# A third width of pass for the small experts of a mixture-of-experts decoder layer, with bias rows loaded first and other edits

## The chip, the cores and the metric

The kernel runs on one core of one Trainium2 chip. The metric is the device time of one execution in microseconds; the median of three runs of the kernel before is 1851.08 us (1849.51 to 1851.67).

## The reference

One decoder layer over 512 tokens of width 1024: a token mixer (an mLSTM branch and a latent-attention branch, gated and merged), cross-attention into 256 memory tokens, and a mixture of experts, each followed by a LayerNorm of `alpha * x + f(x)`. The change lies in the mixture of experts and in the last LayerNorm. Cut to that:

```python
logits = x @ w_router + b_router                    # 512 x 32 experts
top_val, top_idx = top_k(logits, 4);  gate = softmax(top_val)
for each expert e, over the tokens that chose it:
    gu  = x_e @ w_gu[e] + b_gu[e]                   # 1024 -> 2048, two halves: gate and linear
    glu = min(gu_gate, 7);  lin = clip(gu_lin, -7, 7)
    act = glu * sigmoid(1.702 * glu) * (lin + 1)
    y[tokens] += gate_e * (act @ w_dn[e] + b_dn[e]) # 1024 -> 1024
out = layer_norm(alpha * x + y) * ln3_g + ln3_b
```

All weights are float32. How many tokens an expert gets depends on the data and is known only at run time.

## The kernel before, in words

The kernel runs the dense part (mixer, attention, router) first, to about 600 us, then the experts one after the other (`experts`, L1250 to L1347), to about 1811 us, then the last LayerNorm (`finish`, L1465).

Weights. An expert has 24 slabs of 512 KB: 16 for up (8 slices of 128 input channels, by two halves, gate and linear) and 8 for down. SP issues their loads in the order of their use (`slab`, L186) into a ring of 36 buffers: 3 (`raw`) and 6 (`whi`, `wlo`) that the dense part used before, and 8, 14 and 5 more (`NRAW`). A load is issued when its buffer is free, so SP runs ahead of the matmuls by up to 36 slabs.

Tokens. An expert's tokens stand in slots 0 to 191. GpSimd gathers their rows from DRAM (128 into `xg`, up to 64 more into `mrxg`); `tokens` transposes them on TensorE and ScalarE copies them to `xe` (64, then 64 if there are over 64, then 64 if over 128). Over 192 tokens go another way (`overflow`), which these data don't need.

Passes. TensorE holds the tokens as the stationary operand and streams the weights, 512 columns a matmul. A pass is one sweep over some slabs for a group of slots. A pass of 64 slots puts two matmuls side by side on two column tiles of 64; a pass of 32 slots puts four on four column tiles of 32 (`four`, and `down_32`). In float32 each matmul of the program appears as two MATMUL and two LDWEIGHTS records, and each pass of eight matmuls as x16.

`up` (L1104 to L1127) works through four quarters of two slices each. In every quarter there is a pass for slots 0 to 63, and then, nested in conditions on the count `rv`, slots 64 to 95 (L1119), 96 to 127 (L1121) and 128 to 191 (L1123):

```python
self.up_part(e, ks, 64, x[:, :, 0:64], w, two(b))
with tc.If(rv > 64):
    self.up_part(e, ks, 32, x[:, :, 64:96], w, four(b[2]))
    with tc.If(rv > 96):
        self.up_part(e, ks, 32, x[:, :, 96:128], w, four(b[3]))
        with tc.If(rv > 128):
            self.up_part(e, ks, 64, x[:, :, 128:192], w, two(bm))
```

In the last quarter each pass also adds the bias rows by a matmul (`bias`, L1090) with `bgu`, a split of the biases into three bfloat16 parts. `down` (L1182) has two halves of four slices each, nested in the same way (L1189, L1191, L1193). `hidden` turns the activated rows back (L1153 to L1168, conditions at L1162 and after).

Order. The order of the work on TensorE, VectorE, ScalarE and GpSimd is written out by hand (`manual_schedule`). In round e: up of expert e; behind its first quarter `hidden` of expert e-1, behind its third quarter the slots of expert e+2 (`route_expert`, small matmuls on `sl`, L1007 and L1010); then down of expert e-1, in whose middle the activation of expert e (`units`, on VectorE and ScalarE) and the token transposes of expert e+1 stand, with the gather for e+2; then `rows_out` of expert e-1 (VectorE and ScalarE write the result to one of two buffers `ysb`, GpSimd scatters and adds it to `based` in DRAM, L1031). SP's loads are not in that order by hand; they follow the ring.

Conditions. PE's sequencer executes a condition as a compare-and-branch, which the profile shows at the line after the `If` (L1119, L1189 and so on) as PEldq. If the arm is skipped, the sequencer jumps over its instructions.

Start of the stretch. SP issues 24 slabs, then the eight loads of the bias rows (`bias_rows`, L1230), then the other slabs. VectorE and ScalarE turn them into `bgu`, with seven steps one after the other per half. ScalarE's queue also issues the last four stores of `based` (L1048), and ScalarE makes the first token copy.

End. `finish` loads `based` in four blocks; each block's LayerNorm takes sums with bn_stats and bn_aggr on VectorE (L661, L662), the root on GpSimd, a scaling on ScalarE (L667), and two products and two additions by halves (L669, L670); the additions of blocks 0 and 2 run on GpSimd (`FP`), the others on VectorE.

Of the kernel before, what the change touches and what calls it, by code (L numbers as in the profile page):

```python
# [9 lines left out]
F32 = mybir.dt.float32  # L10
# [101 lines left out]
class Trunk:  # L112
# [541 lines left out]

    def layer_norm(self, z, out, gb, add=None, keep=False):

        nc = self.nc
        st = self.pst.tile([128, 2, 6], F32, name="bn", tag="bn")
        mv = self.pst.tile([128, 4], F32, name="mv", tag="mv")
        for i in range(2):  # L660
            nc.vector.bn_stats(st[:, i, :], half(z, i))  # L661
        nc.vector.bn_aggr(mv[:, 0:2], st)  # L662
        self.rstd_col(mv[:, 2:3], mv[:, 1:2])
        nc.vector.scalar_tensor_tensor(mv[:, 3:4], mv[:, 0:1], -1.0, mv[:, 2:3], op0=OP.mult, op1=OP.mult)
        for i in range(2):
            v = half(z, i)
            nc.scalar.activation(v, v, AF.Identity, bias=mv[:, 3:4], scale=mv[:, 2:3])  # L667
            u = half(out, i) if keep else v
            nc.vector.tensor_mul(u, v, half(gb[0], i))  # L669
            (add or nc.vector).tensor_add(half(out, i), u, half(gb[1], i))  # L670

# [401 lines left out]
    def tokens(self, rv):  # L1073

        nc, tc = self.nc, self.tc
        x = self.mx.tile([128, 8, 192], F32, name="xe", tag="xe", bufs=1)

        def some(c, n, src, first=0):
            nc.scalar.copy(x[:, :, c:c + n], self.turned(src, 8, "xt", first).rearrange("p (k t) -> p k t", t=n))  # L1079

        some(0, 64, self.xg[0:64])
        with tc.If(rv > 64):  # L1082
            some(64, 64, self.xg[64:128], 64)
            with tc.If(rv > 128):
                some(128, 64, self.more_x)
        return x
# [17 lines left out]
    def up(self, rv, e, x, w, between):  # L1104

        tc = self.tc
        b = [self.ps("gu", "gu") for _ in range(4)]
        bm = [self.ps("gux", "y") for _ in range(2)]

        def two(b):  # L1110
            return lambda h, j: b[j][64 * h:64 * h + 64]

        def four(b):
            return lambda h, j: b[64 * j + 32 * h:64 * j + 32 * h + 32]

        for q in range(4):
            ks = (2 * q, 2 * q + 1)
            self.up_part(e, ks, 64, x[:, :, 0:64], w, two(b))
            with tc.If(rv > 64):  # L1119
                self.up_part(e, ks, 32, x[:, :, 64:96], w, four(b[2]))  # L1120
                with tc.If(rv > 96):  # L1121
                    self.up_part(e, ks, 32, x[:, :, 96:128], w, four(b[3]))
                    with tc.If(rv > 128):  # L1123
                        self.up_part(e, ks, 64, x[:, :, 128:192], w, two(bm))
            for work in between.get(q, ()):
                work()
        return b, bm  # L1127
# [9 lines left out]
    def units(self, rv, b, bm, twice, between):  # L1137

        tc = self.tc
        g = self.mx.tile([128, 512], F32, name="mg", tag="mg", bufs=1)  # L1140
        l, l2, lx = [self.mx.tile([128, 512], F32, name=n, tag=n, bufs=1) for n in ("ml", "ml2", "mlx")]
        with tc.If(rv > 128):
            self.some_units(g, lx, *bm)
        self.some_units(g, l, b[0], b[1], twice)
        between()
# [6 lines left out]
    def hidden(self, rv, l, l2, lx):  # L1152
# [7 lines left out]

        some(0, 64, l)
        with tc.If(rv > 64):  # L1162
            some(64, 32, l2[0:64])
            with tc.If(rv > 96):  # L1164
                some(96, 32, l2[64:128], 64)
                with tc.If(rv > 128):
                    some(128, 64, lx)
        return hs  # L1168
# [13 lines left out]
    def down(self, rv, h, w, middle):  # L1182
# [3 lines left out]
        for q in range(2):  # L1186
            ks = range(4 * q, 4 * q + 4)
            self.down_64(ks, y, h[:, :, 0:64], w)
            with tc.If(rv > 64):  # L1189
                self.down_32(ks, y2, h[:, :, 64:96], w)  # L1190
                with tc.If(rv > 96):  # L1191
                    self.down_32(ks, y3, h[:, :, 96:128], w)
                    with tc.If(rv > 128):  # L1193
                        self.down_64(ks, yx, h[:, :, 128:192], w)
            if q == 0:
                middle()
        return y, y2, y3, yx

    def rows_out(self, rv, few, p, route):

        nc, tc = self.nc, self.tc
        self.ys.reverse()
        y = self.ys[0]
        yx = self.mx.tile([64, 1024], F32, name="ysx", tag="ysx", bufs=1)
        gate = route[0][1]
# [7 lines left out]

        with tc.If(rv > 64):
            with tc.If(rv > 96):
                with tc.If(rv > 128):
                    for n in range(2):
                        t = yx[:, ts(n, 512)]
                        nc.scalar.copy(t, p[3][64 * n:64 * n + 64])
                        nc.scalar.mul(t, t, route[1][1])  # L1220
                sums(slice(96, 128), p[2])
            sums(slice(64, 96), p[1])
        nc.vector.tensor_copy(y[0:64, 0:512], p[0][0:64])
        nc.scalar.copy(y[0:64, 512:1024], p[0][64:128])  # L1224
        self.scatter(y, route[0][0])
# [3 lines left out]
    def bias_rows(self):  # L1229
# [3 lines left out]
        for h in range(2):  # L1233
            raw = p.tile([128, 2, 512], F32, name="bguraw", tag=("ysx", "hs")[h], bufs=1)
            for i in range(4):
                nc.sync.dma_start(raw[32 * i:32 * i + 32], self.a["bgu"][:, ts(h, 1024)].rearrange("e (j c) -> e j c", j=2))
            nc.vector.tensor_scalar(raw[:, 1], raw[:, 1], 1.0, None, op0=OP.add)
            t = p.tile([128, 2, 512], BF, name="bgu", tag="bgu", bufs=2)
            nc.scalar.copy(t, raw)
            for first in (32, 64):  # L1240
                for r in (slice(a, a + 32) for a in range(first, 96, 32)):
                    nc.vector.tensor_sub(raw[r], raw[r], t[r])
                    nc.scalar.copy(t[r], raw[r])
            self.bgu.append(t)

    def cond(self, c, *engines):
# [3 lines left out]
    def experts(self):  # L1250
        nc, tc, a = self.nc, self.tc, self.a
        p, cond = self.mx, self.cond
        PE, DVE, ACT, POOL = (mybir.EngineType.PE, mybir.EngineType.DVE, mybir.EngineType.Activation, mybir.EngineType.Pool)
        self.more_x = p.tile([64, 1024], F32, name="mrxg", bufs=1)
        nc.vector.memset(self.more_x, 0.0)
        self.ys = [p.tile([128, 1024], F32, name=f"ysb{i}", bufs=1) for i in range(2)]
        for y in self.ys:
            nc.vector.memset(y, 0.0)

# [21 lines left out]
        def more_gather(e):  # L1281
            with tc.If(rv[e][2] > 128):
                self.gather(self.more_x, route[e][1][0])

# [64 lines left out]
    def overflow(self):  # L1349
# [4 lines left out]
        with tc.If(rv > CAP):  # L1354
# [52 lines left out]
            with tc.For_i(0, total, 1):  # L1407
# [52 lines left out]
                y = p.tile([128, 1024], F32, name="oy", tag="ysx", bufs=1)  # L1460
                for n in range(2):
# [3 lines left out]
    def finish(self):  # L1465
        nc, tc, a = self.nc, self.tc, self.a
        with tc.tile_pool(name="fin", bufs=1, reuse_waits="tile") as p:
# [9 lines left out]
    FP = 0, 2  # L1477

    NRAW = 8, 14, 5
    W0, KF, MID = 2, 0, 6  # L1480
# [43 lines left out]
```

## Time and profile before

| | |
|---|---|
| median of 3 runs | 1851.08 us |
| the profiled execution | 1848.75 us, its span 1847.0 us |
| granted TensorE clock, mean of the span | 0.977 |
| PE, matmul | 1673.8 us busy, 91% |
| VectorE | 625.5 us, 34% |
| ScalarE | 469.8 us, 25% |
| GpSimd | 293.9 us, 16% |
| DMA | 504.87 MB, mean 273 GB/s |

The span is the profiled execution from its first instruction to its last; 1.75 us of that execution lie around it. The busy shares are means over the dense part, the experts and the end, which differ: in most of the expert stretch the DMA engines move 350 to 400 GB/s, in the dense part between 69 and 225 for most of it. A row of the timeline gives the start, the busy time, the engine, the line and the tiles, the count of instructions in a run of equal ones, and in brackets the idle time before it with what ended it.

### The profile page before, as it was taken

Reading aid. Unit: us, or ns where it says so; the run is one execution under the profiler, and the core shown is the slowest. Engines: PE = TensorE matmul, PEld = TensorE weight load, DVE = VectorE, ACT = ScalarE, POOL = GpSimd, SP = SyncE. Lnnn points to the kernel's source line nnn. Section 1 sums busy time; section 2 is a strip of 40 time slices with the busy share of each in tenths; the row PEclk is TensorE's granted clock in tenths of the full one; section 3 lists DMA queues with packets and bytes.
Section 4 is the critical chain, followed back from the end, with each engine's and each line's share of the span. In section 5 each row is a group of like instructions: output and inputs, shape, how many; then the busy total and the mean of one; then the engine's idle time right before and its main releaser. Section 6 shows DMA issues by size and latency. Waiting matters only on the chain. (4 is left out here: it accounts for less than half of the span.)

```text
span 1847.0 us, 26521 instructions
## 1 busy us (share of the span) xinstructions
PE 1673.8 (91%) x9564; PEld 853.2 (46%) x9564; DVE 625.5 (34%) x1322; ACT 469.8 (25%) x906; POOL 293.9 (16%) x402
## 2 busy tenths in 40 slices
PE   8999999999999688999999989899999999999991
PEld 7766877868987333333333333333333333333330
DVE  7855777567565411111111211111112102121114
ACT  5577655335443211101101201110101101111001
POOL 1010002421002211211101121111111211011102
PEclk9999999999999799999999999999999999999996
DMA  5223323675236999999858899999999999678973
GB/s 171 91 69 109 105 81 123 221 225 173 83 123 219 351 391 346 396 374 383 305 186 267 325 375 395 364 372 382 392 401 382 376 392 354 229 284 328 399 270 120
DMA packets 149256, 504.87 MB, mean 273 GB/s; under 512 B 21648, under 2 KB 24240, under 8 KB 149040
## 3 DMA queue, kind: packets, MB, share of 16 engines
q1 hardware_dynamic: 131152, 459.33, 66.2%
q0 software_dynamic: 17024, 40.97, 7.6%
q8 instruction: 149, 2.44, 0.5%
q10 hardware_dynamic: 864, 1.57, 0.2%
q14 instruction: 67, 0.55, 0.1%
HBM read 486.84 MB, written 33.29 MB: 282 GB/s over the span
## 5 line engine op out<-in xcount | busy, mean ns | idle before, releaser
L1098 PE MATMUL gu<-raw,xe 128*64 128x512 f32 (+1 forms) x2624 | 518.0, 601 | 27.8 <-PEq L1191 5.1
L1098 PEld LDWEIGHTS gu<-raw,xe 128*64 128x64 f32 (+1 forms) x2624 | 158.2, 127 | 319.8 <-issue 292.9
L1173 PE MATMUL y<-raw,hs 128*64 128x512 f32 x920 | 211.1, 597 | 17.1 <-PEq L1121 4.3
L1133 ACT ACTIVATE mg<-mg 128x512 f32<-128x512 f32 (+1 forms) x55 | 34.7, 630 | 528.8 <-DVE mg L1132 524.4
L1012 DVE TENSOR_REDUCE gs<-sl 128x1 f32<-128x3 f32 x32 | 5.1, 161 | 478.3 <-PE sl L1010 478.3
L998 POOL TENSOR_SCALAR oh<-places,pm 128x192 bf16<-128x192 bf16 x128 | 98.7, 800 | 387.9 <-PE sl L1010 375.8
L1173 PEld LDWEIGHTS y<-raw,hs 128*64 128x64 f32 x920 | 71.1, 136 | 126.5 <-issue 91.1
L130 DVE TENSOR_TENSOR wlo<-raw,whi 128x1024 fp32r<-128x1024 f32 (+2 forms) x81 | 86.9, 1075 | 45.8 <-ACT whi L130 45.3
L1031 POOL DMA_INDIRECT based<-ysb,ixm x32 | 51.5, 1611 | 292.5 <-ACT ysb L1224 280.2
L130 ACT CAST whi<-raw 128x1024 fp32r<-128x1024 f32 (+2 forms) x81 | 75.3, 932 | 81.9 <-issue 17.3
L1098 PE MATMUL gu<-wlo,xe 128*64 128x512 f32 (+1 forms) x368 | 87.5, 594 | 3.1 <-PEq L1164 1.7
L1098 PE MATMUL gu<-whi,xe 128*64 128x512 f32 (+1 forms) x336 | 79.3, 599 | 7.5 <-DVE ysb L1211 2.1
L1025 POOL DMA_INDIRECT xg<-x2d,ixm x32 | 35.9, 1121 | 313.3 <-PEq L1082 179.3
L1132 DVE TENSOR_SCALAR mg<-gu 128x512 f32<-128x512 f32 (+1 forms) x52 | 35.8, 688 | 126.9 <-PE gu L1090 122.8
L1079 ACT COPY xe<-xt 128x512 f32<-128x512 f32 x50 | 27.8, 588 | 190.5 <-PE xt L1070 190.5
L1180 PE MATMUL y<-raw,hs 128*32 128x512 f32 x440 | 57.6, 598 | 0.0
L1211 DVE TENSOR_TENSOR ysb<-ysb,y 32x512 f32<-32x512 f32 x30 | 20.4, 680 | 103.1 <-ACT ysb L1210 103.0
L162 PE MATMUL g<-xTh,wlo 128*128 128x512 f32 x128 | 52.1, 407 | 2.8 <-DVE wlo L130 2.8
L1158 ACT COPY hs<-ht 128x512 f32<-128x512 f32 (+1 forms) x55 | 26.5, 510 | 106.8 <-PEq L1162 56.2
L160 PE MATMUL g<-xTh,whi 128*128 128x512 f32 x128 | 52.2, 408 | 0.0
L161 PE MATMUL g<-xTl,whi 128*128 128x512 f32 x128 | 51.8, 405 | 0.0
L1098 PEld LDWEIGHTS gu<-wlo,xe 128*64 128x64 f32 (+1 forms) x368 | 25.2, 125 | 49.0 <-issue 47.1
(495 smaller groups left out, 2776.9 us busy)
## 6 DMA issues: line engine op xcount, KB each, us to landing
raw<-in_wgu SPq DMA_DIRECT2D x406, 512.0 KB
raw<-in_wdn SPq DMA_DIRECT2D x230, 512.0 KB
wlo<-in_wgu SPq DMA_DIRECT2D x53, 512.0 KB
whi<-in_wgu SPq DMA_DIRECT2D x53, 512.0 KB
raw<-in_wt SPq DMA_DIRECT2D x27, 512.0 KB
whi<-in_wdn SPq DMA_DIRECT2D x13, 512.0 KB
wlo<-in_wdn SPq DMA_DIRECT2D x13, 512.0 KB
tgd<-tg POOLq DMA_DIRECT2D x16, 256.0 KB, 3.5
```

Source lines behind the costliest of these rows:

```text
L130: return nc.scalar.copy(hi, src).ins, (lo_eng or nc.vector).tensor_sub(lo, src, hi.bitcast(F32)).ins
L160: mm(out, w[0], x[0], start=start, stop=False)
L161: mm(out, w[0], x[1], start=False, stop=False)
L162: mm(out, w[1], x[0], start=False, stop=stop)
L998: self.nc.gpsimd.tensor_scalar(oh[:, b], self.places, self.pm[:, b, e:e + 1], None, op0=OP.is_equal)
L1025: return self.nc.gpsimd.indirect_dma_start(out=xg, out_offset=None, in_=self.x2d, in_offset=bass.IndirectOffsetOnAxis(ap=ix[:, 0:1], axis= ...
L1031: self.nc.gpsimd.indirect_dma_start(out=self.based, out_offset=bass.IndirectOffsetOnAxis(ap=ix[:, 0:1], axis=0), in_=y, in_offset=None, bo ...
L1098: mm(out(h, j), x[:, k], w(h, k)[:, ts(j, 512)], start=k == 0, stop=False)
L1132: nc.vector.tensor_scalar(g, pg, 7.0, None, op0=OP.min)
L1133: nc.scalar.activation(g, g, AF.Gelu_apprx_sigmoid)
L1173: self.nc.tensor.matmul(o[64 * n:64 * n + 64], h[:, k], w(k)[:, ts(n, 512)], start=k == 0, stop=k == 7)
L1180: self.nc.tensor.matmul(o[r:r + 32], h[:, k], w(k)[:, ts(n, 512)], start=k < 2, stop=k > 5)
```

## The change

In `up`, `hidden`, `units`, `down` and `rows_out` the work for the first 64 slots now stands in a condition `rv > 32`, with the further conditions nested in it; its other arm handles 32 slots in one pass on four column tiles. Beyond 128 slots, up and hidden go by two groups of 32 (the second under `rv > 160`) instead of one of 64; down still does 64 there. The gather beyond 128 goes to rows 64 to 127 of a tile of 128 rows, `more`, whose rows 0 to 63 take the results beyond 128. There is one `ysb` instead of two. The ring has 38 slabs instead of 36. The bias rows are loaded on ScalarE's queue, ahead of all slabs, the first half into `ysb`. In the last LayerNorm blocks 1 and 3 take their sums on ScalarE, with two activations that accumulate (`sums`), and all additions run on VectorE.

```diff
@@ layer_norm
-        for i in range(2):
-            nc.vector.bn_stats(st[:, i, :], half(z, i))
-        nc.vector.bn_aggr(mv[:, 0:2], st)
+        if stats:
+            stats(mv, z, out)
+        else:
+            for i in range(2):
+                nc.vector.bn_stats(st[:, i, :], half(z, i))
+            nc.vector.bn_aggr(mv[:, 0:2], st)
...
-            (add or nc.vector).tensor_add(half(out, i), u, half(gb[1], i))
+            nc.vector.tensor_add(half(out, i), u, half(gb[1], i))
+
+    def sums(self, mv, z, scratch):
+        nc = self.nc
+        nc.scalar.activation(scratch, z, AF.Identity, accum_out=mv[:, 0:1])
+        nc.vector.tensor_scalar(mv[:, 3:4], mv[:, 0:1], -1.0 / 1024, None, op0=OP.mult)
+        nc.scalar.activation(scratch, z, AF.Square, bias=mv[:, 3:4], accum_out=mv[:, 1:2])
+        nc.vector.tensor_scalar(mv[:, 0:1], mv[:, 3:4], -1.0, None, op0=OP.mult)
+        nc.vector.tensor_scalar(mv[:, 1:2], mv[:, 1:2], 1.0 / 1024, None, op0=OP.mult)
@@ tokens
-                some(128, 64, self.more_x)
+                some(128, 64, self.more[64:128], 64)
@@ up
-            self.up_part(e, ks, 64, x[:, :, 0:64], w, two(b))
-            with tc.If(rv > 64):
-                self.up_part(e, ks, 32, x[:, :, 64:96], w, four(b[2]))
-                with tc.If(rv > 96):
-                    self.up_part(e, ks, 32, x[:, :, 96:128], w, four(b[3]))
-                    with tc.If(rv > 128):
-                        self.up_part(e, ks, 64, x[:, :, 128:192], w, two(bm))
+            with tc.If(rv > 32) as some:
+                self.up_part(e, ks, 64, x[:, :, 0:64], w, two(b))
+                with tc.If(rv > 64):
+                    self.up_part(e, ks, 32, x[:, :, 64:96], w, four(b[2]))
+                    with tc.If(rv > 96):
+                        self.up_part(e, ks, 32, x[:, :, 96:128], w, four(b[3]))
+                        with tc.If(rv > 128):
+                            self.up_part(e, ks, 32, x[:, :, 128:160], w, four(bm[0]))
+                            with tc.If(rv > 160):
+                                self.up_part(e, ks, 32, x[:, :, 160:192], w, four(bm[1]))
+            with some.Else():
+                self.up_part(e, ks, 32, x[:, :, 0:32], w, four(b[0]))
@@ units
         with tc.If(rv > 128):
-            self.some_units(g, lx, *bm)
-        self.some_units(g, l, b[0], b[1], twice)
+            nc.vector.memset(lx[64:128], 0.0)
+            self.some_units(g[0:64], lx[0:64], bm[0][0:64], bm[0][64:128])
+            with tc.If(rv > 160):
+                self.some_units(g[64:128], lx[64:128], bm[1][0:64], bm[1][64:128])
+        with tc.If(rv > 32) as some:
+            self.some_units(g, l, b[0], b[1], twice)
+        with some.Else():
+            self.some_units(g[0:64], l[0:64], b[0][0:64], b[0][64:128])
@@ hidden
-        some(0, 64, l)
-        with tc.If(rv > 64):
...
-                with tc.If(rv > 128):
-                    some(128, 64, lx)
+        with tc.If(rv > 32) as more:
+            some(0, 64, l)
+            with tc.If(rv > 64):
...
+                    with tc.If(rv > 128):
+                        some(128, 32, lx[0:64])
+                        some(160, 32, lx[64:128], 64)
+        with more.Else():
+            some(0, 32, l[0:64])
@@ down
-            self.down_64(ks, y, h[:, :, 0:64], w)
-            with tc.If(rv > 64):
...
+            with tc.If(rv > 32) as some:
+                self.down_64(ks, y, h[:, :, 0:64], w)
+                with tc.If(rv > 64):
...
+            with some.Else():
+                self.down_32(ks, y, h[:, :, 0:32], w)
@@ rows_out
-        self.ys.reverse()
-        y = self.ys[0]
-        yx = self.mx.tile([64, 1024], F32, name="ysx", tag="ysx", bufs=1)
+        y, yx = self.ys, self.more[0:64]
...
+        with some.Else():
+            sums(slice(0, 32), p[0])
@@ bias_rows
-            raw = p.tile([128, 2, 512], F32, name="bguraw", tag=("ysx", "hs")[h], bufs=1)
+            raw = p.tile([128, 2, 512], F32, name="bguraw", tag="hs", bufs=1) if h else self.ys.rearrange("p (j c) -> p j c", j=2)
             for i in range(4):
-                nc.sync.dma_start(raw[32 * i:32 * i + 32], self.a["bgu"][:, ts(h, 1024)].rearrange("e (j c) -> e j c", j=2))
+                nc.scalar.dma_start(raw[32 * i:32 * i + 32], self.a["bgu"][:, ts(h, 1024)].rearrange("e (j c) -> e j c", j=2))
...
+        nc.vector.memset(self.ys, 0.0)
@@ experts
-        self.more_x = p.tile([64, 1024], F32, name="mrxg", bufs=1)
-        nc.vector.memset(self.more_x, 0.0)
-        self.ys = [p.tile([128, 1024], F32, name=f"ysb{i}", bufs=1) for i in range(2)]
-        for y in self.ys:
-            nc.vector.memset(y, 0.0)
+        self.more = p.tile([128, 1024], F32, name="more", bufs=1)
+        self.ys = p.tile([128, 1024], F32, name="ysb", bufs=1)
+        nc.vector.memset(self.more, 0.0)
...
-        fetch(24)
         self.bias_rows()
-        fetch(n - 24)
+        fetch(n)
@@ finish
-                self.layer_norm(z, out[b], gb, nc.gpsimd if b in self.FP else None)
+                self.layer_norm(z, out[b], gb, stats=self.sums if b % 2 else None)
...
-    NRAW = 8, 14, 5
+    NRAW = 8, 14, 7
```

## Rows read from the trace of the kernel before

**Rows 1.** Busy time of the engines over the span (share), instructions.

```profile
PE 1673.8 (91%) x9564; PEld 853.2 (46%) x9564; DVE 625.5 (34%) x1322; ACT 469.8 (25%) x906; POOL 293.9 (16%) x402
```

**Rows 2.** Windows: PE, PEld, DVE, ACT, POOL busy; PE clock, DMA share, GB/s.

```profile
1000.00:1050.00 50.00, 47.02 (x287) 15.78 (x283) 11.61 (x21) 8.84 (x15) 5.91 (x7) 1.00 0.80 286
...
1250.00:1300.00 50.00, 44.86 (x274) 16.55 (x268) 8.64 (x21) 5.24 (x10) 9.87 (x12) 1.00 1.00 383
```

**Rows 3.** PE's waits, what for: us in total, times, longest.

```profile
PE gu L1090 <- ACT bgu L1243: 10.9, 2, 6.6
...
PE ht L1070 <- PEq L1119: 5.0, 16, 0.5
...
PE ht L1070 <- PEq L1121: 4.1, 7, 0.7
...
PE y L1173 <- DMA raw<-in_wdn: 3.1, 8, 0.5
```

**Rows 4.** Timeline of SP's queue, 1440 to 1462 us.

```profile
1455.73 5.70 SPq L186 DMA_DIRECT2D raw<-in_wgu  x4
```

**Rows 5.** Timeline of PE, 1455 to 1490 us.

```profile
1459.68 1.94 PE L1098 MATMUL gu<-whi,xe 128*64 128x512 f32 x8 [0.30 <-DMA raw<-in_wgu]
```

**Rows 6.** Timeline of PE, 1484 to 1500 us.

```profile
1487.14 7.22 PE L1098 MATMUL gu<-raw,xe 128*64 128x512 f32 x48 [0.31 <-PEq L1189]
1494.30 3.65 PE L1098 MATMUL gux<-raw,xe 128*64 128x512 f32 x16
```

**Rows 7.** ScalarE's token copies, from the costliest groups.

```profile
L1079 ACT COPY xe<-xt 128x512 f32<-128x512 f32 x50 | 27.8, 588 | 190.5 <-PE xt L1070 190.5
```

**Rows 8.** Timeline of PE, 1265 to 1330 us.

```profile
1292.95 3.65 PE L1173 MATMUL y<-raw,hs 128*64 128x512 f32 x16
1296.54 1.92 PE L1180 MATMUL y<-raw,hs 128*32 128x512 f32 x16
```

**Rows 9.** Branches at L1119, all and 1092 to 1094: ns min/median/max.

```profile
L1119 PEldq COMPARE_BRANCH  x128: 65/208/3248, 618.0 to 1789.2; - x128
...
L1119 PEldq COMPARE_BRANCH  x1: 3248/3248/3248, 1092.7 to 1092.7; - x1
```

**Rows 10.** Timeline of SP's queue, 530 to 660 us.

```profile
618.74 4.38 SPq L1236 DMA_DIRECT2D bguraw<-in_bgu  x8
```

**Rows 11.** Timeline of ScalarE, 600 to 660 us.

```profile
610.13 4.43 ACTq L1048 DMA_DIRECT2D based<-x2g  x4
614.81 0.59 ACT L1079 COPY xe<-xt 128x512 f32<-128x512 f32 x1 [4.48 <-PE xt L1070]
...
632.89 1.04 ACT L1239 CAST bgu<-bguraw 128x1024 bf16<-128x1024 f32 x1 [17.50 <-DVE bguraw L1237]
```

**Rows 12.** Timeline of GpSimd at the end, 1805 to 1848 us.

```profile
1836.72 3.26 POOL L670 TENSOR_TENSOR fo<-fz,gain 128x512 f32<-128x512 f32 x2 [0.93 <-DVE fz L669]
```

**Rows 13.** Timeline of VectorE at the end, 1810 to 1848 us.

```profile
1838.96 1.58 DVE L670 TENSOR_TENSOR fo<-fz,gain 128x512 f32<-128x512 f32 x1
...
1841.17 0.69 DVE L670 TENSOR_TENSOR fo<-fz,gain 128x512 f32<-128x512 f32 x1
```

**Rows 14.** DMA issues of the scatter: count, median us to landing.

```profile
based<-ysb,ixm POOLq DMA_INDIRECT x32, 9.2
```

**Rows 15.** Timeline of PE, 1088 to 1113 us.

```profile
1092.60 3.65 PE L1098 MATMUL gu<-raw,xe 128*64 128x512 f32 x16 [0.30 <-PEq L1189]
1096.55 1.01 PE L1070 MATMUL ht<-ident,ml 128*128 128x128 f32 x8 [0.30 <-PEq L1119]
```

**Rows 16.** Instruction queue in 650 to 1810, 1093 to 1112, 1094 to 1111: packets, MB, share.

```profile
q8 instruction: 123, 2.02, 0.7%
...
q8 instruction: 4, 0.07, 1.4%
...
q8 instruction: 2, 0.03, 0.8%
```

More of the change, by code (lines that the diff above doesn't have):

```diff
@@ L653, in gains, with layer_norm @@
         return t
-    def layer_norm(self, z, out, gb, add=None, keep=False):
+    def layer_norm(self, z, out, gb, keep=False, stats=None):
         nc = self.nc
@@ L1137, in units @@
     def units(self, rv, b, bm, twice, between):
-        tc = self.tc
+        nc, tc = self.nc, self.tc
         g = self.mx.tile([128, 512], F32, name="mg", tag="mg", bufs=1)
@@ L1159, in some @@
                            self.turned(src, 4, "ht", first).rearrange("p (j h t) -> p j h t", j=4, h=2))
-        some(0, 64, l)
-        with tc.If(rv > 64):
-            some(64, 32, l2[0:64])
-            with tc.If(rv > 96):
-                some(96, 32, l2[64:128], 64)
-                with tc.If(rv > 128):
-                    some(128, 64, lx)
+        with tc.If(rv > 32) as more:
+            some(0, 64, l)
+            with tc.If(rv > 64):
+                some(64, 32, l2[0:64])
+                with tc.If(rv > 96):
+                    some(96, 32, l2[64:128], 64)
+                    with tc.If(rv > 128):
[3 more added lines that the diff above has]
+            some(0, 32, l[0:64])
         return hs
@@ L1187, in down @@
             ks = range(4 * q, 4 * q + 4)
-            self.down_64(ks, y, h[:, :, 0:64], w)
-            with tc.If(rv > 64):
[L1190 to L1194, printed above, removed]
+            with tc.If(rv > 32) as some:
+                self.down_64(ks, y, h[:, :, 0:64], w)
+                with tc.If(rv > 64):
+                    self.down_32(ks, y2, h[:, :, 64:96], w)
+                    with tc.If(rv > 96):
+                        self.down_32(ks, y3, h[:, :, 96:128], w)
+                        with tc.If(rv > 128):
+                            self.down_64(ks, yx, h[:, :, 128:192], w)
+            with some.Else():
+                self.down_32(ks, y, h[:, :, 0:32], w)
             if q == 0:
@@ L1212, in sums @@
             nc.vector.tensor_scalar(y[r], y[r], gate[r], None, op0=OP.mult)
[L1214 to L1224, printed above, removed]
+        with tc.If(rv > 32) as some:
+            with tc.If(rv > 64):
+                with tc.If(rv > 96):
+                    with tc.If(rv > 128):
+                        for n in range(2):
+                            t = yx[:, ts(n, 512)]
+                            nc.scalar.copy(t, p[3][64 * n:64 * n + 64])
+                            nc.scalar.mul(t, t, route[1][1])
+                    sums(slice(96, 128), p[2])
+                sums(slice(64, 96), p[1])
+            nc.vector.tensor_copy(y[0:64, 0:512], p[0][0:64])
+            nc.scalar.copy(y[0:64, 512:1024], p[0][64:128])
+        with some.Else():
+            sums(slice(0, 32), p[0])
         self.scatter(y, route[0][0])
@@ L1282, in more_gather @@
             with tc.If(rv[e][2] > 128):
-                self.gather(self.more_x, route[e][1][0])
+                self.gather(self.more[64:128], route[e][1][0])
         def routing(e):
@@ L1459, in overflow @@
                         nc.tensor.matmul(py[n], h[:, k], w[:, ts(n, 512)], start=k == 0, stop=k == 7)
-                y = p.tile([128, 1024], F32, name="oy", tag="ysx", bufs=1)
+                y = self.ys
                 for n in range(2):
@@ L1473, in finish @@
                 nc.sync.dma_start(z, self.based[ts(b, 128), :])
-                self.layer_norm(z, out[b], gb, nc.gpsimd if b in self.FP else None)
+                self.layer_norm(z, out[b], gb, stats=self.sums if b % 2 else None)
                 nc.sync.dma_start(self.out[ts(b, 128), :], out[b])
-    FP = 0, 2
-    NRAW = 8, 14, 5
+    NRAW = 8, 14, 7
     W0, KF, MID = 2, 0, 6
```

## The prediction, before the change was run

> **What bounds the kernel now.** I read the page's busy times first: TensorE (PE) works in 1673.8 of 1847.0 us, no other engine in over half [rows 1]. [...] PE's waits for the down weights sum to 3.1 us in the whole run, 0.5 at longest; its only long waits are the two for the bias rows, 10.9 us together; the rest are short ones behind its own branches (PEq) [rows 3]. Weights arrive early: SP issues the first up weights of expert 24 at 1455.73, and PE reaches them at 1487.14, 31 us later, a few of which are the transfer itself [rows 4, 6]. I take a lead of 28. So PE sets the pace, and a pass taken away is worth its own time as long as that lead lasts and nothing on PE's queue takes its place.
>
> How long one expert takes is read from starts: expert 23's up begins at 1459.68 and expert 24's at 1487.14, so 27.5 us for an expert of at most 64 tokens [rows 5, 6].
>
> **How often each branch is taken.** The trace shows 50 token copies: 32 first, 15 second, 3 third [rows 7]. So 15 experts have over 64 tokens, 3 of them over 128. How the 17 others split at 32 no row shows; the reference's router, worked out with its inputs, gives six of at most 32 (experts 10, 15, 17, 18, 25, 30) and eleven of 33 to 64, and puts 131, 144 and 147 in the three largest, all under 160.
>
> **What the change takes from PE.** A pass of 64 rows lasts 3.65 us and one of 32 1.92, starts 3.59 apart after the former [rows 8]: 1.73 us a pass. A small expert has six such passes (four in up, two in down): 6 x 6 x 1.73 = 62.3 us. The three largest run their third up pass, 3.65 us as well [rows 6], at 32 rows: 3 x 4 x 1.73 = 20.8.
>
> **What it adds to PE.** Every expert goes through one more branch in seven places (four up quarters, hidden, two down halves). A branch costs about 0.07 us not taken and 0.21 taken (the ends of 65 and 208 ns) [rows 9]. The 26 experts over 32 fall through: 26 x 7 x 0.07 = 12.7. The eleven of 33 to 64 also leave the arm by a jump: waits behind one jump are 0.31 us (5.0/16), behind a nested one 0.58 (4.1/7) [rows 3], so 0.27 x 7 x 11 = 20.8. Small ones jump: 0.21 x 7 x 6 = 8.8. The largest skip the pass beyond 160 (0.56 x 4 x 3 = 6.7) and turn hidden rows in two copies (3). Together 52.
>
> **The bias rows.** Today their eight loads go out on SP at 618.74, behind 24 slabs, ScalarE converts from 632.89, and PE waits 10.9 us for the last of it [rows 3, 10, 11]. Ahead of the slabs they land earlier; but the chain of casts and subtractions keeps its length. I take 8 of the 10.9. The other end is a loss: now ScalarE's queue issues them, 4.38 us of issue today on SP, behind its stores of the base rows (from 610.13, 4.43 us) [rows 10, 11], and ahead of the first token copy, for which PE waits; the two together, some 8 us late, are the bound.
>
> **The end.** GpSimd's last two adds take 3.26 us while the same add on VectorE takes 1.58 beside them and 0.69 alone [rows 12, 13]. Without them VectorE gets four adds more and half the sums less; ScalarE's two full passes lengthen the last block's chain. I take a gain of 2, bounds 3 either way (two of the GpSimd adds' 1.63).
>
> **Edits at nothing.** One output buffer instead of two: a scatter lands 9.2 us (median) after its issue [rows 14], and the shortest expert will still last about 18; were it late, VectorE's writing of the rows would wait, and PE only when the PSUM tiles are wanted again, two halves on. The branches in the units and in the writing of rows run on VectorE and ScalarE beside down passes; two more slabs in the ring only add lead, and SP's later slabs, 4.38 us earlier without the bias loads [rows 10], add to it too.
>
> So far: 62.3 + 20.8 + 8 + 2 - 52 = 41 us gained, 1848.75 - 41 = 1808.
>
> **The term that turns it.** The longest branch record is 3248 ns, at 1092.7, against a median of 208 [rows 9]. It costs nothing today: the pass issued just before it, at 1092.60, runs 3.65 us, and PE is idle 0.30 afterwards [rows 15]. What it waits for shows among the DMA queues: the instruction queue moves 123 pages of 16 KB in 31 experts, 4.0 each, run or skipped; from 1093 to 1112 it moves 4 and without the outer microsecond at both ends 2, so three steps in 17 to 19 us, 5.7 to 6.3 us a page while the weights fill the DMA engines [rows 16]. I take 5.75. The code of an expert grows: up has six passes for four, down five for four, so 6 x 32 + 5 x 16 = 272 matmuls for 192; with transposes and routing unchanged, 4.0 pages become about 5.4, and an expert can't be shorter than 5.4 x 5.75 = 31.1 us. A small one has 27.5 - 10.4 + 1.5 = 18.6 us of work: 12.5 short, 75 over six. One of 33 to 64 has 27.5 + 7 x 0.34 = 29.9: 1.2 short, 13 over eleven. Larger ones have time enough. Gross 88. Off goes what expert 10 would pay, since the DMA share is 0.80 where it runs [rows 2], 12.5, and some 10 for pages in hand where a small one follows a large one. I take 65; the bounds are 0 and 88.
>
> [...]
>
> **The sum:** 1848.75 - 41 + 65 = 1873 for the profiled execution. The median of the runs is 2.3 above that execution, so 1875.
>
> **Rivals.**
> *Pages arrive in time* (the other side). For it: every fetch so far is hidden, and a stalled PE stops taking slabs, so that SP stops issuing and pages come faster. Against it: small experts run through pages in 3.4 us (18.6/5.4), under the 5.7 measured. The time is 1810 against the median. It decides at 18.6/5.4: with a page under 3.4 us nothing is exposed.
> *Pages come at 5.0 us.* The floor is 27, only small ones pay, 8.4 each, five of them, less the 10: 32. Then -41 + 32 = -9: 1842.
> *The full price*, no page in hand: -41 + 88 = +47: 1898.
> *The weights become the bound.* Only where fetches are hidden: experts 15, 17, 18 and 21 to 23 draw faster than the DMA engines refill. An expert is 24 slabs of 512 KB, 12.6 MB, at 383 GB/s [rows 2] 33 us; each small one takes 14 us off the lead of 28, two in a row all of it; some 5 us lost: 1815.
> *It doesn't do what it says*: no expert takes the short arm at run time. Then the 62.3 are gone and the six pay 0.34 instead of 0.21 in seven places: -41 + 62 + 5 = +26: 1877, and more with the fetches.
>
> **How the numbers follow.** A measurement can tell 0.2% (3.7 us). Chances: forecast 0.44 (1858 to 1890), pages in time 0.26, half 0.16 (0.10 of it faster, 0.06 within), full price 0.10, weights 0.03 (0.02 faster, 0.01 within), the last 0.01 (slower). Faster 0.26 + 0.10 + 0.02 = 0.38, same 0.06 + 0.01 = 0.07, slower 0.44 + 0.10 + 0.01 = 0.55. The range reaches from pages in time to the full price, 1807 to 1898; only the outer parts of both lie beyond. The likeliest case's own is 1858 to 1890.
>
> **What would show it.** Right: branch records of several us at the new outer conditions of up and down, PE idle behind them, the instruction queue near 123 x 5.4/4.0 = 166 pages in the expert stretch, small experts about 31 us from start to start, those of 33 to 64 about 30 to 31, passes of 1.92 in the small ones, the bias wait gone down to 3. Wrong: small experts at 19 us, or PE waiting for weights behind experts 18 and 23, or the new branches no longer than 0.21 us.

## The result, and the profile after the change

The changed kernel takes 1916.41 us (median of 4 runs, 1915.08 to 1922.99) against 1850.46 before: a ratio of 1.0362, 95% interval 1.0347 to 1.0377. It is 66 us slower; the prediction had the sign, but 1875 and a range up to 1898.

The page's busy times, clock slices (tenths of full speed, 40 slices) and instruction queue (packets, MB, share):

```profile
PE 1618.4 (85%) x9576; PEld 814.2 (43%) x9576; DVE 629.7 (33%) x1340; ACT 476.2 (25%) x923; POOL 286.8 (15%) x398
...
PEclk9999999999997899999999899997999999999986
...
q8 instruction: 198, 3.24, 0.7%
```

PE has 55 us less to do than before [rows 1], in a span 66 us longer: 121 us of new idle time. What ends it, PE's waits say:

```profile
PE gu L1110 <- DMA raw<-in_wdn: 21.9, 18, 3.2
PE gu L1110 <- DMA raw<-in_wgu: 19.3, 19, 4.3
PE gu L1110 <- issue: 18.6, 24, 3.4
PE gu L1110 <- ACTq L1094: 16.3, 1, 16.3
...
PE y L1201 <- PEq L1133: 7.5, 7, 2.0
...
PE ht L1082 <- PEq L1135: 5.5, 7, 1.1
```

The two largest groups name weights, and one would go looking for a full DMA queue. That is the trap of this profile. Expert 17's up (22 tokens) shows it:

```profile
1302.98 3.64 PE L1110 MATMUL gu<-raw,xe 128*32 128x512 f32 x16 [4.30 <-DMA raw<-in_wgu]
...
1309.33 3.41 PE L1110 MATMUL gu<-raw,xe 128*32 128x512 f32 x16 [1.04 <-DMA raw<-in_wgu]
1315.12 3.03 PE L1110 MATMUL gu<-raw,xe 128*32 128x512 f32 x16 [2.38 <-DMA raw<-in_wdn]
...
1320.87 3.64 PE L1110 MATMUL gu<-raw,xe 128*32 128x512 f32 x16 [1.98 <-DMA raw<-in_wdn]
```

Its up can't be waiting for down weights (`in_wdn`): the named transfers only landed last before the matmul started. The sequencer's branch records say more (minimum, median, maximum in ns; first and last start). L1131 and L1216 stand behind the new condition `rv > 32` in up and in down, L1133 behind `rv > 64`; the last line is L1131 in this stretch alone:

```profile
L1131 PEldq COMPARE_BRANCH  x128: 70/73/6053, 616.1 to 1858.0; - x128
...
L1133 PEldq COMPARE_BRANCH  x148: 65/176/5112, 629.3 to 1862.4; - x148
...
L1216 PEldq COMPARE_BRANCH  x64: 65/73/5482, 682.5 to 1873.7; - x64
...
L1131 PEldq COMPARE_BRANCH  x4: 442/3670/5873, 1296.8 to 1318.9; - x4
```

The branch that starts at 1296.8 lasts 5873 ns, so it ends at 1302.7, and the first matmul follows at 1302.98. The sequencer stood in the jump to the short arm. What it stood for shows in the packets of the instruction queue in the same trace. Pages of 16 KB start at 1300.19, 1305.91, 1312.47, 1318.26 and 1324.00, so 5.7 to 6.6 us apart, four of them within this up:

```profile
q8 instruction: 4, 0.07, 1.3%
```

The three long jumps end at 1302.71, 1314.95 and 1320.71, each 2.5 us after the start of a page. That is no chance: of the 35 branch records over 2 us in the changed kernel every one ends 2.3 to 2.5 us after such a start. The long branches wait for code.

Over the expert stretch 48 branch records exceed 0.7 us, 151.8 us together; before there were 20, 34.9 us together, at most 3248 ns [rows 9].

Three windows of that same up compare its length (columns as in [rows 2]). The changed kernel:

```profile
1302.98:1324.87 21.89, 16.49 (x93) 4.74 (x93) 0.55 (x5) 0.93 (x2) 4.65 (x6) 0.58 1.02 398
```

The same up in the kernel before:

```profile
1299.02:1316.73 17.71, 16.29 (x88) 6.31 (x89) 3.78 (x10) 1.83 (x4) 4.65 (x6) 1.00 1.03 390
```

And in the kernel `e2_all_wide` below, in which this expert runs the wide arm:

```profile
1304.87:1327.28 22.41, 18.37 (x93) 6.57 (x93) 1.28 (x7) 1.44 (x3) 4.65 (x6) 0.92 1.03 398
```

Narrow passes make it 4.2 us longer than before, not 7 us shorter, and wide ones in the same code take half a microsecond more. There, too, the pages of this up come 5.8 us apart, four in its 22.41 us. The granted clock also fell: 0.58 on the mean, 0.50 from 1302.14 to 1312.38 and from 1315.79 to 1326.03, and the passes take 3.0 to 3.6 us, where a pass of expert 18's up, at 1343.12 and a clock of 1.00, takes 1.92. When it fell, at 1302.14, PE had stood idle since 1298.68, the first 3.5 us of the 4.30 before this up.

### The profile page after: what moved, and what is told of

It is laid out like the page before. It is cut to its first block, busy times and chain, and to the rows that moved or that the text cites. A ratio compares the mean times of both kernels' runs of the same rounds, so it can differ in the third digit from the quotient of the medians.

```text
span 1913.0 us, 27182 instructions
## 1 busy us (share of the span) xinstructions
PE 1618.4 (85%) x9576; PEld 814.2 (43%) x9576; DVE 629.7 (33%) x1340; ACT 476.2 (25%) x923; POOL 286.8 (15%) x398
## 5 line engine op out<-in xcount | busy, mean ns | idle before, releaser
L1110 PE MATMUL gu<-raw,xe 128*64 128x512 f32 (+1 forms) x2716 | 542.1, 639 | 104.8 <-DMA raw<-in_wdn 19.5
L1151 ACT ACTIVATE mg<-mg 64x512 f32<-64x512 f32 (+1 forms) x55 | 34.6, 630 | 602.0 <-DVE mg L1150 597.9
L1201 PE MATMUL y<-raw,hs 128*64 128x512 f32 x676 | 157.1, 603 | 30.5 <-DMA raw<-in_wgu 9.8
L1201 PEld LDWEIGHTS y<-raw,hs 128*64 128x64 f32 x676 | 49.8, 139 | 118.2 <-issue 96.5
L1208 PE MATMUL y<-raw,hs 128*32 128x512 f32 x544 | 73.5, 623 | 13.6 <-issue 4.9
L1110 PE MATMUL gu<-wlo,xe 128*32 128x512 f32 (+1 forms) x304 | 72.1, 603 | 10.3 <-DMA raw<-in_wgu 2.7
L1110 PE MATMUL gu<-whi,xe 128*32 128x512 f32 (+1 forms) x308 | 71.5, 598 | 3.0 <-DMA raw<-in_wdn 1.2
L1240 DVE TENSOR_TENSOR ysb<-ysb,y 32x512 f32<-32x512 f32 x42 | 28.5, 680 | 133.1 <-ACT ysb L1239 132.8
L162 PE MATMUL g<-xTh,wlo 128*128 128x512 f32 x128 | 52.5, 410 | 2.8 <-DVE wlo L130 2.8
L1182 ACT COPY hs<-ht 128x256 f32<-128x256 f32 (+1 forms) x58 | 25.5, 469 | 115.9 <-PE ht L1082 70.8
L1082 PE MATMUL ht<-ident,ml 128*128 128x128 f32 (+1 forms) x208 | 28.1, 262 | 26.5 <-issue 8.8
```

The source lines that it names most:

```text
L162: mm(out, w[1], x[0], start=False, stop=stop)
L1110: mm(out(h, j), x[:, k], w(h, k)[:, ts(j, 512)], start=k == 0, stop=False)
L1151: nc.scalar.activation(g, g, AF.Gelu_apprx_sigmoid)
L1201: self.nc.tensor.matmul(o[64 * n:64 * n + 64], h[:, k], w(k)[:, ts(n, 512)], start=k == 0, stop=k == 7)
L1208: self.nc.tensor.matmul(o[r:r + 32], h[:, k], w(k)[:, ts(n, 512)], start=k < 2, stop=k > 5)
```

## The experiments

**Where the 66 us lie.** From the starts of up and down on PE in both timelines, summed by the expert they belong to, between the start of the third up and that of the last: experts of at most 32 tokens +9.6, of 33 to 64 +41.3, of 65 to 128 +20.3, over 128 -8.3; the start of the stretch brings 5.2, the last up and downs -1, the end -1. (The classes count only what lies between those two starts: nine of the eleven experts of 33 to 64, for instance.) My theory was the code pages; the rivals were the narrow passes themselves and the weights.

**Code that never runs.** `e7_before_dead_code`, the kernel before with

```diff
                         self.up_part(e, ks, 64, x[:, :, 128:192], w, two(bm))
+                        with tc.If(rv > 192):
+                            self.up_part(e, ks, 32, x[:, :, 128:160], w, four(bm[0]))
+                            self.up_part(e, ks, 32, x[:, :, 160:192], w, four(bm[1]))
...
                         self.down_64(ks, yx, h[:, :, 128:192], w)
+                        with tc.If(rv > 192):
+                            self.down_32(ks, y3, h[:, :, 160:192], w)
```

> The kernel before, with two more passes of 32 in every up quarter and one in every down half, innermost in the nest under rv > 192, which no expert reaches: as much code as the changed kernel has, none of it run. Theory 'pages': TensorE's sequencer gets its code page by page, 5 to 6 us each, whether it is run or jumped over, so the 17 experts of at most 64 tokens go from 27.5 to some 31 us, and what idles them may lower the clock: 1890 to 1920 us against 1850 before. Rivals 'narrow passes' (the passes of 32 slow TensorE down) and 'weights' (small experts outrun the loads): nothing that runs is changed but three more branches in the largest experts, 1848 to 1855 us.

It takes 1888.24 against 1850.08: ratio 1.0212 (1.0193 to 1.0232), 38 us for code that no expert reaches. The branches in front of it (minimum, median, maximum in ns):

```profile
L1119 PEldq COMPARE_BRANCH  x128: 65/212/6116, 617.0 to 1828.8; - x128
```

The instruction queue's pages in 650 to 1850 us:

```profile
q8 instruction: 165, 2.70, 0.9%
```

The longest record doubles [rows 9] and the pages grow from 123 to 165 [rows 16]. Rivals that need a narrow pass or a faster draw on weights can't make this; the size is just under what was expected. Not all of it is dead code: 9.8 us lie in the three largest experts, which evaluate the new condition, and 31 in the others, which never reach it.

**The change without its short arms.** `e1_no_small` removes every `rv > 32` with its Else:

```diff
-            with tc.If(rv > 32) as some:
-                self.up_part(e, ks, 64, x[:, :, 0:64], w, two(b))
...
-            with some.Else():
-                self.up_part(e, ks, 32, x[:, :, 0:32], w, four(b[0]))
+            self.up_part(e, ks, 64, x[:, :, 0:64], w, two(b))
...
```

> The changed kernel without its condition rv > 32 and without the short arms, all else as changed. Pages: up has five passes of code and down four, 4.0 x 224/192 = 4.7 pages an expert or 27 us, just under the 27.5 that the work takes, so hardly a stall shows: 1851 + 5 at the start - 12.5 in the three largest = 1840 to 1850 us, branch records no longer than about 4 us, clock 1.00 behind 700 us. Narrow passes and weights expect the same here; if it stays above 1890, all three are wrong and the cause lies in the edits that this kernel keeps.

1845.46, ratio 0.997 (0.9958 to 0.9983). The largest experts are 12.8 us shorter, the others 9 longer. One expectation failed: records of up to 5437 ns remain at its first condition (L1132), yet PE's waits behind it are 1.8 us at longest for `y`, 0.7 for `sl` and 0.3 for `ht`, with a wide pass of 3.65 us in front. So the loss of 66 comes with the short arms.

**Same code, no narrow pass.** `e2_all_wide`:

```diff
-            with tc.If(rv > 32) as some:
+            with tc.If(rv > 0) as some:
```
(in all five places)

> The changed kernel with rv > 0 in place of rv > 32: the same code to the instruction, but the six small experts run the wide arm, and no short pass runs. Pages: the code still sets 31 us and more for every expert of at most 64 tokens, so it is about as slow as the changed kernel or slower: 1910 to 1935 us, with long branch records and a lowered clock. Narrow passes and weights: the loss of the small experts goes, what stays are branches and jumps of 26 + 6 experts (about 1.5 us each, 48), the start (5) and the largest (-12.5): 1885 to 1895 us, clock 1.00.

1928.70, ratio 1.0425 (1.0406 to 1.0444): 79 us over the kernel before, 12 over the changed one. That rules out the narrow passes as the cause: they gain, but 12 us instead of the 62.3 of work they remove, and most of it in down (five downs take 37.8 us for 48.8). Up of the small experts lasts 21.6 us here on the mean and 21.0 in the changed kernel: something sets it that hardly asks how long the passes are, and the pages' starts say what. The run also bears on what the clock costs. Over the stretch it is 0.99 here (window 650 to 1830):

```profile
650.00:1830.00 1180.00, 1004.69 (x6290) 344.19 (x6288) 186.07 (x395) 132.15 (x236) 175.30 (x207) 0.99 0.89 333
```

The same window of the changed kernel has 0.96:

```profile
650.00:1830.00 1180.00, 974.86 (x6310) 325.78 (x6312) 195.28 (x408) 134.66 (x242) 174.53 (x205) 0.96 0.90 335
```

In expert 17's up of the changed kernel the second pass, at a clock of 0.55, ends at 1312.7, while the jump that began beside it at 1309.4 lasts to 1314.95: there the lower clock falls into time that the page takes anyway. Expert 18's up says the same from the other side:

```profile
1339.28:1359.88 20.60, 10.19 (x88) 3.21 (x89) 4.86 (x12) 2.16 (x4) 4.65 (x6) 0.92 1.02 376
```

At a clock of 0.92 PE works in half of it, and yet it lasts 20.6 us, against 19.8 with wide passes in `e2_all_wide`. What the clock costs elsewhere was not separated.

**The branches without the code.** `e10_one_level`, the kernel before with one more level:

```diff
-            self.up_part(e, ks, 64, x[:, :, 0:64], w, two(b))
+            with tc.If(rv > 0) as some_:
+                self.up_part(e, ks, 64, x[:, :, 0:64], w, two(b))
...
+            with some_.Else():
+                self.tc.nc.tensor.matmul(four(b[0])(0, 0), x[:, ks[0], 0:32], w(0, ks[0])[:, 0:512], start=ks[0] == 0, stop=False)
```
(in down alike; in hidden the other arm is `some(0, 32, l[0:64])`)

> The kernel before with its nests in up, hidden and down put in one more condition, rv > 0, whose other arm holds a single matmul (in hidden, one short copy) and never runs: the branches and jumps of the change without its code. The prediction priced them at 0.34 us a place in an expert of 33 to 64 and 0.07 in larger ones: 7 x (0.34 x 17 + 0.07 x 15) = 48 us, 1898, if nothing hides them. The changed kernel's trace suggests more in the larger experts (20 us over twelve of 65 to 128) and that part of the 41 over the eleven is not jumps but pages: 1885 to 1905. If the jumps are cheap and it is all pages: under 1870.

1912.16, ratio 1.0338 (1.0322 to 1.0354): 62 us, above all that was expected. It is the largest single price in this case, and neither pages nor clock make it. The pages of the whole stretch (650 to 1870 us) are 129 for 123 [rows 16]:

```profile
q8 instruction: 129, 2.11, 0.7%
```

The branch records over 0.7 us even sum to less than before, 20.5 us for 34.9, and the clock is 1.00. The waits behind PE's own branches show it, as in [rows 3]:

```profile
PE sl L1007 <- PEq L1120: 8.9, 16, 0.6
...
PE ht L1070 <- PEq L1122: 7.1, 10, 0.8
...
PE ht L1070 <- PEq L1120: 6.1, 9, 0.7
```

Behind the shallow branch the wait for `ht` is 0.68 us (6.1/9) where it was 0.31, behind the nested one 0.71 where it was 0.58 [rows 3]. By the starts of the rounds an expert of at most 64 tokens pays 2.8 us, 0.40 in each of seven places, a larger one 1.0, or 0.14.

Why the two differ shows in the branch records of up. The first line is of the kernel before, the others of `e10_one_level`; L1121 and L1122 stand behind the same condition, `rv > 96`:

```profile
L1121 PEldq COMPARE_BRANCH  x100: 65/176/433, 655.8 to 1737.3; - x100
...
L1118 PEldq COMPARE_BRANCH  x128: 70/73/78, 616.1 to 1848.3; - x128
L1120 PEldq COMPARE_BRANCH  x196: 65/176/2619, 616.4 to 1852.7; - x196
L1122 PEldq COMPARE_BRANCH  x100: 65/176/434, 656.5 to 1791.5; - x100
```

Every expert passes the new branch, L1118. Behind `rv > 64` there are 196 records for 128 before [rows 9], 68 more: the 17 experts of at most 64 tokens now leave by a second jump of 176 ns in each of four quarters. Behind `rv > 96` nothing is new: larger experts left their nest by such a jump before. The jump out isn't hidden. In expert 17's third quarter the last matmul ends at 1308.84 and the jump starts at 1309.03, and the wait behind it grows from 0.30 us (first line, kernel before) to 0.54:

```profile
1311.51 0.46 PE L1007 MATMUL sl<-VT,oh 128*128 128x8 bf16 x8 [0.30 <-PEq L1119]
...
1309.37 0.46 PE L1007 MATMUL sl<-VT,oh 128*128 128x8 bf16 x8 [0.54 <-PEq L1120]
```

An estimate from these: 0.24 us for the jump out in 17 x 7 places, and 0.13 for the branch in front (a larger expert pays 0.14 a place for it) in 32 x 7, make 58 of the 60.5 us by which the two spans differ.

**A pass of code less.** `e9_no_160`:

```diff
                             self.up_part(e, ks, 32, x[:, :, 128:160], w, four(bm[0]))
-                            with tc.If(rv > 160):
-                                self.up_part(e, ks, 32, x[:, :, 160:192], w, four(bm[1]))
```
(and in the activation)

> The changed kernel without the pass beyond 160 slots in up (and its activation), which no expert of these data reaches: five passes of code in up instead of six, five in down, 4.0 x 240/192 = 5.0 pages an expert. Pages: the floor falls from 31.1 to 28.8 us, 2.3 us in each of some 15 experts, and one branch of the three largest goes: 1875 to 1890 us. Rivals (narrow passes, weights): 6 us of branches at most, 1908 to 1916.

1883.59, ratio 1.0193 (1.0176 to 1.0209): 33 us faster than the changed kernel for the removal of a pass that no expert ran and of a branch in three experts. The sum of the price came out, its split less so: by the starts on PE the small experts are 19.5 us shorter than in the changed kernel and those of 33 to 64 8, but the three largest, for which only a branch was priced, 15, and the start takes 6 back.

**Half the weight traffic.** In both kernels

```diff
-                slabs[e, part, k] = self.slab(a["wdn"][e, k] if part == 2 else a["wgu"][e, part, k])
+                slabs[e, part, k] = slabs[e, part, k - 1] if k % 2 else self.slab(a["wdn"][e, k] if part == 2 else a["wgu"][e, part, k])
```

> The kernel before, but every second slab is not loaded: its neighbour is used in its place, so half of the weight traffic is left out (and the values differ). PE's work and its code are unchanged. All theories: few waits for weights go, 1835 to 1850 us. It is the base for the next kernel.

> The changed kernel with the same half of the weight traffic left out. If a code page takes 5 to 6 us because the weights fill the DMA engines, pages now come in about half of that, the branch records over 2 us all but vanish, the small experts' narrow passes gain what they remove, and the kernel ends near the one before with half the weights: from 35 us under it to 10 over it. If a page takes its time whatever the DMA engines do, it stays some 60 us over it.

The base takes 1846.22, the changed kernel 1871.37. So the difference falls from 66 to 25 us: between the two cases that I had set. The longest branch of the base falls too (before: 3248 [rows 9]):

```profile
L1119 PEldq COMPARE_BRANCH  x128: 65/208/1719, 619.1 to 1787.4; - x128
```

With half the loads the waits are shorter (29 branch records over 0.7 us in the changed kernel, 79.5 us together, for 48 and 151.8), but records up to 6082 ns remain. By itself this run doesn't tell the code from the weights as the cause; the pages' starts above do. Expert 17's up shows why the test was less clean than intended:

```profile
1289.74:1305.66 15.92, 10.98 (x93) 3.60 (x93) 1.88 (x7) 0.86 (x2) 4.65 (x6) 0.89 0.72 237
```

The mean share over the stretch was 0.50, but the loads come in bursts, and here it is 0.72. It takes 15.9 us instead of 21.9. The levels stand in this kernel too; what they cost at this load (62 us in `e10_one_level` at the full one) no run shows. How a page's time depends on the load is left open beyond this sign.

**The bias rows.** `e3_tokens_first` moves the first token copy ahead:

```diff
-        self.bias_rows()
-        fetch(n)
         more_gather(0)
         xs, ls = {0: self.tokens(rv[0][0])}, {}
+        self.bias_rows()
+        fetch(n)
```

> The changed kernel with the first token copy put ahead of the bias rows, both on ScalarE. Theory: the first pass waited 16.3 us because ScalarE's queue held the loads of the bias rows and seven conversions ahead of that copy; now it starts near 614 instead of 629, and the bias wait is at most 5: 8 to 14 us less than the changed kernel, 1902 to 1908. Rival: the first pass was held by its code or its weights, and the bias wait of before (10.9) comes back: 1913 to 1918.

1913.89 (1911.04 to 1916.01), 2.5 less than the changed kernel: the rival's number, though for half of its reason. The copy was what PE waited for, not code or weights, but the saving came back at the bias rows, as the rival had it:

```profile
617.82 4.50 PE L1110 MATMUL gu<-raw,xe 128*64 128x512 f32 x9 [4.83 <-POOL oh L1010]
...
651.40 1.01 PE L1102 MATMUL gu<-bgu,esel 128*64 128x512 bf16 x3 [9.62 <-ACT bgu L1275]
```

PE begins at 617.8 instead of 629.2, and then waits 2.60 and 9.62 us for `bgu`, as before [rows 3]. In the changed kernel the loads went out late although they stand first, and the copy stands behind them and the first half's conversions (ScalarE's timeline):

```profile
616.76 1.91 ACTq L1268 DMA_DIRECT2D ysb<-in_bgu  x4
...
628.59 0.58 ACT L1091 COPY xe<-xt 128x512 f32<-128x512 f32 x1
```

In the kernel before, VectorE's fill of `ysb` shows what holds that buffer: the stores of the base rows (VectorE's timeline).

```profile
619.03 0.91 DVE L1258 MEMSET ysb<- 128x1024 f32 x1 [3.14 <-DMA based<-x2g]
```

So I take it that loads into it can't start much earlier, wherever they stand in the program; no run tests it. `e8_no_small_bias_back` puts the loads back in the kernel without short arms:

```diff
-                nc.scalar.dma_start(raw[32 * i:32 * i + 32], self.a["bgu"][:, ts(h, 1024)].rearrange("e (j c) -> e j c", j=2))
+                nc.sync.dma_start(raw[32 * i:32 * i + 32], self.a["bgu"][:, ts(h, 1024)].rearrange("e (j c) -> e j c", j=2))
...
+        fetch(24)
         self.bias_rows()
-        fetch(n)
+        fetch(n - 24)
```

> The changed kernel without the short arms and with the loads of the bias rows back on SP's queue, behind 24 slabs. With the bias rows ahead, PE's first pass waited 17 us and the bias wait of 10.9 was gone, so putting them back gives 3 to 6 us: 1838 to 1843 against 1850 before. If the order of the bias rows is neutral, 1845.

1844.60, ratio 0.9981 (0.9967 to 0.9994), against 0.997 (0.9958 to 0.9983) for `e1_no_small`: the intervals overlap, so the place of the bias rows is neutral within the measurement. The third up starts 4.0 us later than before in the one and 5.7 in the other.

**Narrow passes that add no code.** `e11_cap_160` takes the idea where it needs no further arm: the kernel before with its third group cut to 32 slots.

```diff
-CAP = 192
+CAP = 160
...
-                        self.up_part(e, ks, 64, x[:, :, 128:192], w, two(bm))
+                        self.up_part(e, ks, 32, x[:, :, 128:160], w, four(bm[0]))
...
-                        self.down_64(ks, yx, h[:, :, 128:192], w)
+                        self.down_32(ks, yx, h[:, :, 128:160], w)
```
(activation, hidden rows and output alike)

> The kernel before with the third group of slots cut from 64 to 32 throughout (128 to 159; an expert over 160 would go the overflow's way): its passes in up and in down are of 32, and no code is added. Pages and jumps are as before, so the narrow passes are worth what they remove: 3 experts x 6 passes x 1.73 = 31 us: 1816 to 1824. If a narrow pass in itself costs the clock or time elsewhere: 1835 or more.

1812.08, ratio 0.9797 (0.9784 to 0.981): 38 us faster than the kernel before and 104 faster than the changed one. Its narrow third passes take 1.90 us:

```profile
947.07 1.90 PE L1098 MATMUL gux<-raw,xe 128*32 128x512 f32 x16
...
954.45 1.90 PE L1180 MATMUL yx<-raw,hs 128*32 128x512 f32 x16
```

So a narrow pass is worth 1.73 us and slightly more (38 us over 18 passes) where no code, branch or page comes with it. (An expert of 161 to 192 tokens would pay more, by the overflow's way; these data have none over 147.)

## Why the prediction was wrong in size

**What holds.** PE's own queue took the passes' place: long records at the new outer conditions (6053 ns in up, 5482 in down), 170 pages in the expert stretch where 166 were forecast, PE idle behind the branches, and every record over 2 us ending 2.3 to 2.5 us behind a page's start. With every page in time the sum was 1808. The record of 5873 ns and `e7_before_dead_code` speak against that, and so do its 31 us in experts that never reach the dead code.

**Term by term**, in the order of the text:
- *Three largest:* forecast -20.8 + 6.7 + 3 and their checks, about -10; measured -8.3. Right in sum, partly by luck: `e9_no_160` puts the pass beyond 160 and its branch nearer 15 us than 6.7, and in `e11_cap_160` these experts gain 36 us by 18 narrow passes, where 31 were to be expected.
- *Experts of 33 to 64:* forecast 20.8 of jumps, 5 of checks and 13 of pages, 39, for eleven; measured 41.3 for nine of them. The sum is near, its parts less so: in `e10_one_level` the level alone costs these nine 25.7, in `e7_before_dead_code` the code alone 19.5, which is 45 together. That the two overlap, since a page can arrive during one more jump, would explain it; no run shows it.
- *Experts of 65 to 128:* forecast 6, the 0.07 us of a branch not taken in each of seven places; measured 20.3. This step failed, by its size. That only "the eleven of 33 to 64 also leave the arm by a jump" anew was right, as the 100 records behind `rv > 96` show (L1121; 100 behind L1135 of the changed kernel too). But the branch in front costs 0.14 us a place, twice its record of 73 ns: 11.4 us in `e10_one_level`. (PE's waits put down to "issue" at an up pass grow there from 0.24 us, 7.1/30, to 0.42, 12.3/29.) Dead code adds 1.5 in `e7_before_dead_code`; the other 7 are open. By the prediction's prices the level of `e10_one_level` comes to 48 us over all 32 experts; it costs 62.
- *Small experts:* forecast -62.3 + 8.8 + 52.5 = -1; measured +9.6, without expert 30's down. "12.5 short" each was right as a mechanism, but the credit of 22.5 for pages in hand and the lighter DMA load at expert 10 was too large, by about half: without it the forecast would have been +21. The 10 in it for pages in hand were an estimate of mine that no run shows by itself. And expert 10's up (19.5 us) was little shorter than the other five's (20.6 to 21.9).
- *Bias rows:* forecast a gain of 8; measured a loss of 5.2 at the start of the third up. This step failed. The bound named the cause (ScalarE's queue ahead of the first token copy, 8 us late), the chosen value was at the wrong end, and the price was larger: PE's first pass starts 13.8 us later (629.2 for 615.4), against 10.9 of bias wait removed. That is a loss of 2.9; another 2.3 is what the levels alone bring by then in `e10_one_level`. Within the measurement the move is worth nothing either way, as `e8_no_small_bias_back` shows for the kernel without short arms; why the third up starts late there too stays open.
- *The end:* forecast -2; measured -1 (35.5 us from the last matmul to the end of the span for 36.5).

13 (bias) + 14 (65 to 128) + 11 (small) + 2 + 2 + 1 = 43, less 1 in the last up and downs: the missing 42 us between 1873 and the profiled 1915. So the mechanism was right, and the terms that failed are the bias rows, the larger experts' branches and the credit for the small ones. The edits at nothing hold as far as the waits show: what PE's waits put down to `ysb` at the start of an up, 7.2 us in the changed kernel with one buffer, is 8.4 in `e10_one_level` with two.

**The clock** was taken as 1.00 throughout, as in [rows 2]. It fell to 0.96 over the expert stretch (650 to 1830 us, where the kernel before has 1.00 from 650 to 1810), in expert 17's case to 0.50 while PE stood idle. That was a step left out. In the small experts' ups it can have changed little: expert 18's, at 0.92, lasts 20.6 us, and expert 17's, at 0.58, 21.9.

**Rivals.** Pages in time falls, and so do pages at 5.0 us: in expert 17's up they start 5.7 to 6.6 apart. The short arms do run. The weights as the bound falls as well: `e7_before_dead_code` and `e10_one_level` lose 38 and 62 us with the DMA traffic slower than before (339 and 336 GB/s from 650 to 1830 us, for 344 from 650 to 1810). The full price, 1898, came nearest, and would have needed the levels and the start to reach 1916.

## What to carry to other kernels

A condition around a hot loop's body had a price here in every iteration, taken or not: 0.14 us for the branch alone and 0.40 with a new jump past its Else, and code under one cost time without being run (38 us in `e7_before_dead_code`). Price it for all iterations, the ones that gain nothing first, and ask whether work can shrink in an arm that is there already. A wait that a profile puts down to a transfer is worth a look at the sequencer's branch records at the same time before one believes it.

## What the runs showed of the hardware that was not expected

- Code that never runs cost time at a distance in `e7_before_dead_code`: two passes more in each quarter of up and one in each half of down, under a condition that only three experts even reach, cost 38 us, 31 of them in the experts that never reach it.
- Branches of PE's sequencer that lasted over 2 us ended 2.3 to 2.5 us after the start of a 16 KB packet on the instruction queue, all 35 in the changed kernel; in expert 17's up such packets started 5.7 to 6.6 us apart.
- A level of If and Else with hardly any code in the Else cost 62 us over 224 places in `e10_one_level`, with 129 pages for 123 and at a clock of 1.00: 0.28 us each on the mean, above the record of the branch itself (0.07); in expert 17's third quarter the jump out began 0.19 us after the last matmul's end.
- In expert 17's up the passes of 32, behind idle times of 1.0 to 4.3 us, took 3.0 to 3.6 us at a granted clock of 0.58 on the mean (1.92 us in expert 18's up at 1.00); the wide passes of `e2_all_wide`, behind idle times of 0.4 to 0.7, had 0.92.
